# A gated linear unit on one core: the store of each tile issued behind the next tile's sigmoid instead of ahead of it

## The chip, the cores and the metric

The kernel runs on one core of one Trainium2 chip. The metric is the device time of one execution, in microseconds (us); lower is better. Beside it, one execution was recorded by the hardware profiler; the views of that record (the page, groups of instructions, waits, the chain of waits, stretches of time) are what the text reads.

## The reference

The input `x` has 8192 x 8192 float32 numbers. It is cut into a left and a right half of 4096 columns, and the left half is multiplied by the sigmoid of the right half:

```python
def reference(x: np.ndarray) -> np.ndarray:
    a, b = np.split(x, 2, axis=-1)
    return a * (1 / (1 + np.exp(-b)))
```

Every input number is read once (268 MB) and every output number written once (134 MB).

## The kernel before

The 8192 rows are cut into 32 tiles of 256 rows, two rows for each of the 128 partitions. A tile of `x` is one load of 8.39 MB (64 KB for each partition); its result is one store of 4.19 MB. There are two input buffers (`x_sb0`, `x_sb1`) and two output buffers (`o_sb0`, `o_sb1`); tile i uses number i mod 2 of each.

Nothing is scheduled by a tool: the order of instructions on each engine is the order in which the code writes them, and all waits are written by hand.

- SyncE issues the loads (`load`, L46 to L51, its DMA in L48). Load i+2 overwrites the input buffer of tile i, so it waits until multiply i is done. SyncE also issues the four part-stores of the last tile.
- ScalarE computes the sigmoid in place in the input buffer (L61) and waits for the load of its tile. ScalarE also issues the stores of tiles 0 to 30 (`store`, L78 to L89, its DMA in L82); store i waits until multiply i is done.
- VectorE multiplies the left half by the sigmoid into the output buffer (L72). Multiply i waits for sigmoid i and, by the same semaphore `ready[s]`, for store i-2, which reads the buffer that it overwrites:

```python
                self.to_ready[s] += 1 + (16 if i >= SLOTS else 0)
                waits.append((self.ready[s], self.to_ready[s]))
```

The first and the last tile are computed in four pieces each; the others in one sigmoid and one multiply. The loop in `trace` (L97 to L102) writes for each tile the sigmoid and the multiply, then load i+2, then the store of tile i. On ScalarE this makes the order sigmoid 0, store 0, sigmoid 1, store 1, and so on: a store's wait for its multiply stands ahead of the next tile's sigmoid.

The loads (SyncE's queue) and the stores (ScalarE's queue) run on the same 16 DMA engines.

Of the kernel before, what the change touches and what calls it, by code (L numbers as in the profile page):

```python
# [1 line left out]

# [4 lines left out]

P = 128
R = 2
SLOTS = 2  # L10


class _Program:

    def __init__(self, nc, x, out):
        self.nc = nc
        fp32 = mybir.dt.float32
        n_rows, n_cols = x.shape
        self.half = n_cols // 2  # L30
        self.n_tiles = n_rows // (P * R)
        self.x = x.rearrange("(n p r) m -> n p (r m)", p=P, r=R)
        self.out = out.rearrange("(n p r) m -> n p (r m)", p=P, r=R)
        self.xs = [nc.alloc_sbuf_tensor(f"x_sb{s}", [P, R * n_cols], fp32).ap() for s in range(SLOTS)]
        self.os = [nc.alloc_sbuf_tensor(f"o_sb{s}", [P, R * self.half], fp32).ap() for s in range(SLOTS)]
        self.loaded = [nc.alloc_semaphore(f"loaded{s}") for s in range(SLOTS)]
        self.ready = [nc.alloc_semaphore(f"ready{s}") for s in range(SLOTS)]
        self.product = nc.alloc_semaphore("product")
        self.sigmoid = nc.alloc_semaphore("sigmoid")
        self.arrived = nc.alloc_semaphore("arrived")  # L40
        self.last = nc.alloc_semaphore("last")
        self.to_ready = [0] * SLOTS
        self.products = self.sigmoids = self.lasts = 0
        self.done = {}

    def load(self, i, after=None):  # L46
        s = i % SLOTS
        ins = self.nc.sync.dma_start(out=self.xs[s][:, :], in_=self.x[i]).then_inc(self.loaded[s], 16)  # L48
        if i >= SLOTS:
            ins._wait_ge(self.product, self.done[i - SLOTS])  # L50
        return ins  # L51

    def work(self, i, pieces):

        nc, s = self.nc, i % SLOTS
        rows = self.xs[s].rearrange("p (r h m) -> p r h m", r=R, h=2)
        packed = self.os[s].rearrange("p (r m) -> p r m", r=R)
        waits = []
        for k, (r, c) in enumerate(pieces):
            b = rows[:, r, 1, c]  # L60
            sig = nc.scalar.activation(out=b, in_=b, func=mybir.ActivationFunctionType.Sigmoid)  # L61
            if k == 0:
                sig._wait_ge(self.loaded[s], 16 * (i // SLOTS + 1))
                self.to_ready[s] += 1 + (16 if i >= SLOTS else 0)
                waits.append((self.ready[s], self.to_ready[s]))
                sig.then_inc(self.ready[s], 1)
            else:
                self.sigmoids += 1
                waits.append((self.sigmoid, self.sigmoids))
                sig.then_inc(self.sigmoid, 1)  # L70
        for (r, c), wait in zip(pieces, waits):
            mul = nc.vector.tensor_mul(out=packed[:, r, c], in0=rows[:, r, 0, c], in1=rows[:, r, 1, c])  # L72
            mul._wait_ge(*wait)
            mul.then_inc(self.product, 1)
            self.products += 1
        self.done[i] = self.products

    def store(self, i, lo=0, hi=None, products=None):  # L78
        s, final = i % SLOTS, i == self.n_tiles - 1
        hi = R * self.half if hi is None else hi  # L80
        queue = self.nc.sync if final else self.nc.scalar
        ins = queue.dma_start(out=self.out[i][:, lo:hi], in_=self.os[s][:, lo:hi])  # L82
        ins._wait_ge(self.product, self.done[i] if products is None else products)
        if final:
            self.lasts += 16
            ins.then_inc(self.last, 16)
        else:
            ins.then_inc(self.ready[s], 16)
        return ins  # L89

    def trace(self):

        n, half = self.n_tiles, self.half
        whole = [(slice(0, R), slice(0, half))]
        fourths = [(slice(r, r + 1), slice(h * half // 2, (h + 1) * half // 2)) for r in range(R) for h in range(2)]
        self.load(1)
        for i in range(n):  # L97
            self.work(i, fourths if i in (0, n - 1) else whole)
            if i + SLOTS < n:
                self.load(i + SLOTS)  # L100
            if i < n - 1:
                self.store(i)  # L102
        for k in range(4):
            self.store(n - 1, k * half // 2, (k + 1) * half // 2, self.products - 3 + k)

    def close(self):


        nc, s = self.nc, (self.n_tiles - 2) % SLOTS
        for engine in (nc.scalar, nc.vector, nc.sync):  # L110
            engine.drain().then_inc(self.arrived, 1)  # L111
        nc.gpsimd.wait_ge(self.arrived, 3)
        nc.gpsimd.wait_ge(self.ready[s], self.to_ready[s] + 16)
        ids = sorted(h.num for h in (*self.loaded, *self.ready, self.product, self.sigmoid, self.arrived))
        assert ids == list(range(ids[0], ids[-1] + 1)) and self.last.num not in ids
        nc.gpsimd.sem_clear(range(ids[0], ids[-1] + 1))
        nc.gpsimd.drain()
        nc.sync.wait_ge(self.last, self.lasts).then_inc(self.last, -self.lasts)


def _launch_early(nc):

    SP = mybir.EngineType.SP
    entry, body = (b.instructions for b in nc.main_func.blocks[:2])
    load = next(i for i in body if i.engine == SP and i.opcode == "DMACopy")
    assert not load.sync_info.on_wait
    body.remove(load)
    where = next(k for k, i in enumerate(entry) if i.engine == SP and i.opcode == "Drain")  # L130
    entry.insert(where, load)


@with_exitstack
def kernel(
    ctx: ExitStack,
    tc: tile.TileContext,
    x: bass.AP,
    out: bass.AP,
):  # L140
    nc = tc.nc
    prog = _Program(nc, x, out)
    tc.info.no_tile_sem_insts.add(prog.load(0).ins.name)
    tc.close()
    tc.compile()  # L145
    _launch_early(nc)
    prog.trace()
    prog.close()


# [1 line left out]
_INS = ['x']  # L152
_OUTS = [((8192, 4096), 'float32')]


# [23 lines left out]
```

## Time and profile before

| what | value |
|---|---|
| time, median of 3 runs | 933.25 us (933.01 to 934.12) |
| the profiled execution: time, span | 933.08 us, 931.8 us |
| VectorE busy | 278.6 us (30%) |
| ScalarE busy | 226.8 us (24%) |
| bytes moved, mean rate over the span | 402.67 MB, 432 GB/s |
| loads, issue to landing (median) | 42.2 us |
| stores on ScalarE's queue, issue to landing (median) | 34.8 us |
| one sigmoid of a whole tile, one multiply | 7.03 us, 8.69 us |

How to read it: the span is the time from the first to the last instruction of the profiled execution; 1.3 us lie around it. "Busy" is the time in which an engine computed. "Issue to landing" counts from the instruction that issues a transfer until the last of its data is reported to have arrived, and so holds the time in which the transfer stood behind others. On the page the queue of SyncE is named q1 and that of ScalarE q10. DMA shares are those of 16 engines together; packets are counted where they end, so in short stretches a share may pass 1.

### The profile page before, as it was taken

Reading aid. Unit: us, or ns where it says so; the run is one execution under the profiler, and the core shown is the slowest. Engines: PE = TensorE matmul, PEld = TensorE weight load, DVE = VectorE, ACT = ScalarE, POOL = GpSimd, SP = SyncE. Lnnn points to the kernel's source line nnn. Section 1 sums busy time; section 2 is a strip of 40 time slices with the busy share of each in tenths; the row PEclk is TensorE's granted clock in tenths of the full one; section 3 lists DMA queues with packets and bytes.
Section 4 is the critical chain, followed back from the end, with each engine's and each line's share of the span. In section 5 each row is a group of like instructions: output and inputs, shape, how many; then the busy total and the mean of one; then the engine's idle time right before and its main releaser. Section 6 shows DMA issues by size and latency. Waiting matters only on the chain.

```text
span 931.8 us, 190 instructions
## 1 busy us (share of the span) xinstructions
DVE 278.6 (30%) x38; ACT 226.8 (24%) x39; POOL 0.2 (0%) x4
## 2 busy tenths in 40 slices
DVE  0333213333133331233312333123331233312333
ACT  1323330233311333113331133311333203332033
POOL 0000000000000000000000000000000000000000
DMA  9999999999999999999999999999999999999999
GB/s 405 428 450 428 422 456 405 450 428 428 450 421 435 428 436 442 428 428 450 450 405 430 442 456 428 412 463 408 450 428 428 450 408 447 428 428 450 426 429 405
DMA packets 9649, 402.67 MB, mean 432 GB/s; under 512 B 1072, under 2 KB 1072, under 8 KB 1072
## 3 DMA queue, kind: packets, MB, share of 16 engines
q1 hardware_dynamic: 5184, 272.63, 67.7%
q10 hardware_dynamic: 4464, 130.03, 32.3%
q14 instruction: 1, 0.01, 0.0%
HBM read 268.44 MB, written 134.22 MB: 432 GB/s over the span
## 4 chain that ended last, share of the span: by engine, by line
DMA 73%; DVE 15%; ACT 12%; DVEq 0%; issue 0%
DMA x_sb<-in_x_dram 73%; DVE o_sb L72 15%; ACT x_sb L61 12%; DVEq L111 0%
## 5 line engine op out<-in xcount | busy, mean ns | idle before, releaser
L72 DVE TENSOR_TENSOR o_sb<-x_sb 128x8192 f32<-128x8192 f32 (+1 forms) x38 | 278.6, 7344 | 647.1 <-ACT x_sb L61 647.1
L61 ACT ACTIVATE x_sb<-x_sb 128x8192 f32<-128x8192 f32 (+1 forms) x38 | 225.5, 5949 | 693.9 <-DMA x_sb<-in_x_dram 693.9
L61 ACT ACT_TABLE_LOAD x1 | 1.3, 1283 | 1.4 <-PEq L145 1.4
L163 POOL MEMSET const-bfloat16-1.0<- 128x1 bf16 x1 | 0.1, 102 | 0.0
L163 POOL MEMSET const-uint8-127<- 128x1 uint8 x1 | 0.1, 102 | 0.0
L163 POOL MEMSET const-float32-0.0<- 128x1 f32 x1 | 0.1, 99 | 0.2 <-issue 0.2
L163 POOL MEMSET const-float32-1.0<- 128x1 f32 x1 | 0.1, 99 | 0.0
## 6 DMA issues: line engine op xcount, KB each, us to landing
out_dram<-o_sb ACTq DMA_DIRECT2D x31, 4096.0 KB, 34.8
out_dram<-o_sb SPq DMA_DIRECT2D x4, 1024.0 KB, 5.7
x_sb<-in_x_dram SPq DMA_DIRECT2D x32, 42.2
```

The source lines that it names most:

```text
L61: sig = nc.scalar.activation(out=b, in_=b, func=mybir.ActivationFunctionType.Sigmoid)
L72: mul = nc.vector.tensor_mul(out=packed[:, r, c], in0=rows[:, r, 0, c], in1=rows[:, r, 1, c])
L163: nc = _bacc.Bacc("TRN2", target_bir_lowering=False, num_devices=1)
```

## The change

In the loop, the store of tile i-1 is written where the store of tile i stood, behind the work of tile i. For i = 30, the last turn that still has a store on ScalarE, both store 29 and store 30 are written. On ScalarE the order becomes sigmoid 0, sigmoid 1, store 0, sigmoid 2, store 1, ..., sigmoid 30, store 29, store 30, sigmoid 31. All waits, buffers, transfers and the order on the other engines are the same. Two blank lines in the class move the line numbers behind them by two.

```diff
@@ -98,7 +100,9 @@
             self.work(i, fourths if i in (0, n - 1) else whole)
             if i + SLOTS < n:
                 self.load(i + SLOTS)
-            if i < n - 1:
+            if 0 < i < n - 1:
+                self.store(i - 1)
+            if i == n - 2:
                 self.store(i)
         for k in range(4):
             self.store(n - 1, k * half // 2, (k + 1) * half // 2, self.products - 3 + k)
```

## The prediction

> **What bounds the kernel now.** I read the page first, parts 1 to 3: who is busy, and how evenly.
>
> ```profile
> DVE 278.6 (30%) x38; ACT 226.8 (24%) x39; POOL 0.2 (0%) x4
> ...
> DMA  9999999999999999999999999999999999999999
> ...
> q1 hardware_dynamic: 5184, 272.63, 67.7%
> q10 hardware_dynamic: 4464, 130.03, 32.3%
> ```
>
> VectorE and ScalarE work less than a third of the span; the 16 DMA engines never fall below nine tenths in any slice. The queue rows sharpen that: the packets of SyncE's queue (q1: all loads and the last tile's stores) take 67.7% of what 16 engines have in the span, those of ScalarE's queue (q10: the stores) 32.3%, together 100.0%. From the same rows, one load of 8.39 MB costs all 16 engines 0.677 x 931.8 x 8.39 / 272.63 = 19.4 us, one store of 4.19 MB 0.323 x 931.8 x 4.19 / 130.03 = 9.7 us: 29.1 us a tile.
>
> The chain of waits seems to say something else: it hops from load to sigmoid to multiply to load.
>
> ```profile
> by line: DMA x_sb<-in_x_dram 72.6%; DVE o_sb L72 14.7%; ACT x_sb L61 11.5%; DVEq L111 0.2%; issue 0.1%
> ...
> 160.74 7.04 ACT x_sb L61
> 167.80 8.70 DVE o_sb L72
> 176.52 42.13 DMA x_sb<-in_x_dram
> 218.67 7.04 ACT x_sb L61
> ```
>
> The loop is real (7.04 + 8.70 + 42.13 = 57.9 us for two tiles, 28.95 each), but the 42 us of a load are not 42 us of moving: 19.4 us would do. The rest is standing behind the load before it and alternating with a store. So the loop closes because the transfers are that slow, and its two compute links cost nothing. The stretches view confirms it between landings (columns: stretch and its length, then DVE, ACT and POOL busy, clock, DMA share, GB/s):
>
> ```profile
> 1.44:21.79 20.35, 0.00 (x0) 1.28 (x1) 0.00 (x0) 1.00 0.95 412
> 21.79:44.76 22.97, 8.90 (x4) 7.31 (x5) 0.00 (x0) 1.00 0.94 388
> ...
> 73.64:102.64 29.00, 8.69 (x1) 7.03 (x2) 0.00 (x0) 1.00 1.00 434
> ...
> 885.90:914.82 28.92, 8.69 (x1) 7.03 (x2) 0.00 (x0) 1.00 0.99 431
> 914.82:931.80 16.98, 8.90 (x4) 7.31 (x4) 0.00 (x0) 1.00 0.94 401
> ```
>
> Share 1.00 in the steady state. Only the ends are short of it (a stretch's share counts packets where they land, so I use it for long stretches): 5% of 20.35 us at the start, 6% of 16.98 us behind the last load, 1.0 us each. The change first acts at 32.66 us, where the store of tile 0 is issued now, so the start stays. What it could still win is about 1 us at the end.
>
> The second stretch also shows how the queues share. Load 1 needs 19.4 us alone and took 22.97; the 3.6 us more are three store packets (a store is 8 packets per engine, 1.21 us each), served between load packets of 2.43 us. The queues alternate packet by packet: while both hold work, loads get two thirds of the time, stores one third, just the ratio of their bytes.
>
> **The change, step by step.** Per tile the same 38 multiplies, 38 sigmoids and 67 DMAs; nothing is added or removed, only ScalarE's order moves: sigmoid i+1 now stands ahead of store i. No scheduler changes that; a listing of both kernels' instructions shows exactly this swap on ScalarE and nothing on the other engines.
>
> *What ScalarE gains.* Sigmoid i+1 no longer queues behind store i's wait for multiply i. It never suffered from it: ScalarE then idled another 21.9 us for the load (its 32 waits for loads sum to 693.9 us). Worth 0.
>
> *What the store loses.* Write T for the landing of load i+1. Now store i is issued 7.06 + 8.72 = 15.8 us behind its own tile's landing, at T - 13.2. After, it is issued behind sigmoid i+1, at T + 7.1: some 20 us later. The store's DMA is the only one that moves; SyncE's queue keeps its waits.
>
> *Start.* Load 1 is alone and lands at 21.79 + 19.4 = 41.2 (now 44.76). Store 0 goes out at 48.3. It reaches the engines 0 to 6.1 us later (the upper bound from store 0 now: issued at 32.66, none of its packets landed by 38.7, the first 16 by 40.1, so it joined at about 38.8). So load 2 runs alone 7.1 to 13.2 us, then at two thirds speed, and lands at 63.7 to 66.8 against 73.64 now: all loads shift 7 to 10 us ahead, and I take 8.5. Engines stay busy meanwhile: load 3 is issued at 41.2 + 15.8 = 57.0. From then each tile again moves one load and one store, 29.0 us.
>
> *The new wait.* Multiply i+2 writes the buffer that store i reads. Now store i lands 34.8 us after its issue, at T + 21.6, while multiply i+2 is due at T + 29.0 + 7.1 = T + 36.1: 14.5 us of slack. After, the same 34.8 us end at T + 41.9: the multiply waits 5.8 us behind its sigmoid. Bounds: 0 if the store takes only its shared 29 us; 12.7 us if it joins as late as 6.1 us. I take 6, by the 34.8 us row. Queued behind that multiply on VectorE is only the next one, 29 us away. Who waits for it: SyncE's load i+4, now issued 13.2 us ahead of the landing of load i+3, when the load queue would run empty; after, 7.2 us ahead. From issue to moving a load needs at most 2.4 us (load 0 lands at 21.79, 19.4 of it moving), so about 5 us of cover remain. At the 12.7 us bound the load queue would run dry for 2 us, and even that costs nothing: store i+1, issued before multiply i+2, holds up to 9.7 us of packets, so the engines then serve stores alone and catch up.
>
> The Trainium skill speaks against the move: the page "DMA: Bandwidth & Descriptors", section "Rules for kernel authors", wants a DMA issued early, compute done, and its semaphore waited on late. By that rule the store's 20 us of lost cover would show as lost time; the row of 100.0% says that delay in one queue is filled from the other.
>
> *End.* The last load lands at about 914.8 - 8.5 = 906.3, but the bytes skipped are still owed. The engines finish at about 931 now; from 906.3 that leaves 24.7 us of work: 9.7 for tile 31, 9.7 for store 30, 5.3 of store 29. Multiply 31 waits for store 29 till about 912.5 and its four pieces end at 921.4 (8.9 us as now); the last piece of the store is issued then (now 925.7) while the backlog lasts to 906.3 + 15.0 = 921.3 without pieces, and pieces 1 to 3 add 7.3 us. No hole opens; the end stays.
>
> Sum: 0 + 0 + 0. The profiled execution took 933.08 us (span 931.8 and 1.3 around it), the median of the runs is 933.25: I predict 933.2. Unknowns of a packet or so at the end: -0.9 to +1.5.
>
> **Rivals.** No change, forecast: 0.88. A change under 0.2% (1.9 us) is about what a measurement here cannot tell from none.
>
> *Slower: the circle through the output buffers runs both queues dry.* Store i lands, multiply i+2 (8.7) and the load's start (2.4) follow: 11.1 us until new load packets, covered by store i+1 (9.7) and the rest of load i+3. By my times that rest is 16 us of shared running, 10.7 us of packets. If it were gone when store i lands, 11.1 - 9.7 = 1.4 us would be idle in each of 29 tiles: 41 us, 974. It decides only if the multiply's wait grows from 6 to about 20 us, say because stores stand back behind queued loads. For: store landings of 34.8 us against 9.7 of work. Against: 34.8 is no more than alternation and the next store's tail. Chance 0.08.
>
> *Slower: the early-issue rule holds literally*, every multiply's 5.8 us lengthening its tile: 29 x 5.8 = 168 us, 1101. Against: the 42.1 us loads have that slack. Chance 0.01.
>
> *Faster: the last tile sets the end.* With the last load 8.5 us earlier and the chain behind it as now, 933.2 - 8.5 = 924.7. For: the chain of waits ends in load, sigmoid and multiply. Against: behind 914.82 the engines still carry 16 us of bytes, 0.94 busy. Chance 0.03.
>
> **How the numbers follow.** The forecast alone holds 0.88, so the range is its own: 933.2 with -0.9 and +1.5, 932.3 to 934.7. Faster 0.03, same 0.88, slower 0.08 + 0.01 = 0.09.
>
> **What would show it.** In the profile after: DMA nines throughout and the two queue shares again near 100%; stores to landing still 30 to 39 us; VectorE with waits for DMA of o_sb, some 6 us on about 29 multiplies (none now); landings about 8.5 us earlier from tile 2 on, still 29.0 us apart; the last load at about 906, the end at about 931.8. A DMA share of 0.95 in the middle, or loads over 30 us apart, would make it wrong towards slower; a span under 930 towards faster.

## The result, and the profile after

The changed kernel takes 949.81 us (median of 4 runs, 946.82 to 951.89) against 933.64 us: 1.0173 times as long, 95% interval 1.0158 to 1.0188. That is 16 us slower: less than 2%, but far clear of the noise. 933.2 had been forecast. The profiled execution took 951.89 us with a span of 950.6 us, 18.8 us more than before.

From its page: engines' busy time, the DMA row of the 40 slices, and the two queues (packets, MB, share of what 16 engines have in the span):

```profile
DVE 278.6 (29%) x38; ACT 226.8 (24%) x39; POOL 0.2 (0%) x4
...
DMA  9999999999999999999999999999999999999995
...
q1 hardware_dynamic: 5184, 272.63, 67.3%
q10 hardware_dynamic: 4464, 130.03, 31.7%
```

Packets and bytes are those of before. But the same loads took longer: 67.3% of 950.6 us are 639.8 us of all engines, against 630.8 before. The stores did not: 31.7% are 301.3 us, against 301.0. And the shares sum to 99.0%, not 100.0%: about 1% of the engines' time, 9.5 us, is empty. The last slice says where most of it is. In stretches between landings (as before: length, busy DVE, ACT, POOL, clock, DMA share, GB/s):

```profile
22.02:41.35 19.33, 8.89 (x4) 7.31 (x5) 0.00 (x0) 1.00 1.00 434
...
70.49:101.10 30.61, 8.69 (x1) 7.03 (x1) 0.00 (x0) 1.00 1.01 432
130.79:160.33 29.54, 8.69 (x1) 7.03 (x1) 0.00 (x0) 1.00 1.00 424
869.70:899.97 30.27, 8.69 (x1) 7.02 (x1) 0.00 (x0) 1.00 1.00 416
...
912.00:929.87 17.87, 3.72 (x1) 0.00 (x0) 0.00 (x0) 1.00 0.86 372
929.87:950.60 20.73, 8.90 (x4) 7.31 (x4) 0.00 (x0) 1.00 0.56 236
```

Load 1 alone lands in 19.33 us, as worked out. From load 3 on a tile takes 29.2 to 30.6 us, where before took about 29.0, and the share stays about 1.00: the engines are busy all the time and move less in it. Only at the end do they wait, 0.86 and 0.56: most have nothing left while the last load still lands.

The timeline (start, length, engine, line, instruction; ACTq is ScalarE issuing a transfer) shows something else that the prediction did not have:

```profile
41.35 7.03 ACT L63 ACTIVATE x_sb<-x_sb 128x8192 f32<-128x8192 f32 x1 [12.02 <-DMA x_sb<-in_x_dram]
41.35 0.38 ACTq L84 DMA_DIRECT2D out_dram<-o_sb  x1
48.41 8.69 DVE L74 TENSOR_TENSOR o_sb<-x_sb 128x8192 f32<-128x8192 f32 x1 [15.55 <-ACT x_sb L63]
70.49 7.03 ACT L63 ACTIVATE x_sb<-x_sb 128x8192 f32<-128x8192 f32 x1 [22.11 <-DMA x_sb<-in_x_dram]
70.50 0.34 ACTq L84 DMA_DIRECT2D out_dram<-o_sb  x1
```

The store behind a sigmoid is issued when the sigmoid STARTS (41.35, 70.50), not when it ends: ScalarE hands the transfer out while the sigmoid still runs. So stores go out at each load's landing.

**Packet by packet.** The trace also records each DMA packet: queue, size, start, duration. It does not number the engines, but packets follow each other within some nanoseconds, so an engine's row can be put together by matching ends to starts. (Where two engines' packets end at the same moment, the match can swap their rows, so sums for one engine are good to about 1 us.) L0 to L7 are the eight 64 KB packets of a load on one engine, S0 to S7 the eight 32 KB packets of a store, `|l|` and `|s|` the small packets that report a load's and a store's end; `*0.34` means that the packet took 0.34 us over its 2.42 us:

```
before, any engine     L5 |s| L6 S0 L7 S1 |l| S2 L0 S3 L1 S4 L2 S5 ...
after, slowest engine  |l| S7 L0 |s| L1*0.34 S0 L2 S1 L3*0.18 S2 L4 ...
after, other engines   |l| S5 L0 S6 L1 S7 L2 |s| L3 S0 L4 S1 L5 ...
```

(The lower two are the same 50 us, from 335 us on.) All the lost time lies in load packets that are drawn out. Past 60 us, 322 of the changed kernel's 3744 load packets take over 0.1 us too long, 0.39 us on average; before, one of 3760 does. Up to 790 us there are 198 of them, and some 170 of these stand where a store ends one load packet behind a load's end. Two engines are in that place in nearly all tiles, a third in some 19; the other 13 are in it for their first two to seven tiles, run ahead, so that a store ends two or three packets later in their row, and are then left in peace. The slowest engine has some 20 us of drawn-out packets from start to end, against some 2 us before; the difference of about 18 us is nearly all of the 18.8. A load has landed only when the slowest engine has it.

The other 124 come in the last tiles and mostly elsewhere. There the engines that ran ahead have emptied their store queue, and the load packet in service when the next store arrives is drawn out by 0.7 to 0.8 us on average (`L5 L6*0.78 S0 L7`). These engines have time to spare: most stand idle for 7 to 8 us before the last stores.

### The profile page after: what moved, and what is told of

It is laid out like the page before. It is cut to its first block, busy times and chain, and to the rows that moved or that the text cites. A ratio compares the mean times of both kernels' runs of the same rounds, so it can differ in the third digit from the quotient of the medians.

```text
span 950.6 us, 190 instructions
## 1 busy us (share of the span) xinstructions
DVE 278.6 (29%) x38; ACT 226.8 (24%) x39; POOL 0.2 (0%) x4
## 3 DMA queue, kind: packets, MB, share of 16 engines
q1 hardware_dynamic: 5184, 272.63, 67.3%
q10 hardware_dynamic: 4464, 130.03, 31.7%
## 4 chain that ended last, share of the span: by engine, by line
DMA 73%; DVE 14%; ACT 11%; DVEq 0%; issue 0%
DMA x_sb<-in_x_dram 73%; DVE o_sb L74 14%; ACT x_sb L63 11%; DVEq L115 0%
## 5 line engine op out<-in xcount | busy, mean ns | idle before, releaser
L63 ACT ACTIVATE x_sb<-x_sb 128x8192 f32<-128x8192 f32 (+1 forms) x38 | 225.5, 5949 | 709.0 <-DMA x_sb<-in_x_dram 709.0
## 6 DMA issues: line engine op xcount, KB each, us to landing
out_dram<-o_sb ACTq DMA_DIRECT2D x31, 4096.0 KB, 33.1
```

## The experiments

Ratios are to the kernel before, run on the same chip, with 95% intervals.

### Is it where the stores start, the compute beside them, or their lateness?

Theory W held that a store queue that has run empty costs at the next arrival; C that compute beside a store's start slows the loads; D that late or separate issue costs. In the first run store 0 alone is issued 7 us later, behind the END of sigmoid 1:

```diff
             if 0 < i < n - 1:
+                if i == 1:
+                    self.nc.scalar.drain()
                 self.store(i - 1)
```

> The changed kernel, but store 0 alone is issued behind the END of sigmoid 1 (a drain of ScalarE in front of it): about 7 us later, once. Theory W (an empty queue costs): when a store's packets reach a DMA engine whose store queue has run empty, the load packet in service is drawn out by some 0.6 us; in the changed kernel each store ends just before the next arrives, so this comes back in all 30 tiles (30 x 0.6 = 18 us). One later store 0 leaves a backlog that lasts: time about 933 to 935, loads 29.0 us apart. Rival C (a store that starts together with a sigmoid disturbs the loads in the buffers): 29 of 30 stores still start with a sigmoid, 947 to 952. Rival D (issuing loads and stores at different moments, or late stores, costs by itself): 947 to 952.

Measured: 933.48 us, 0.9998 (0.9989 to 1.0008). One store, moved once by 7 us, wins the whole loss back. The engines alternate packet by packet, so what the first store sets stays: in this run a store ends four load packets behind a load's end, 300 us on too. D falls.

In the second, sigmoid and multiply work on 64 columns only (`c = slice(c.start, c.start + 64)`, and the output buffers are filled with zeros once, so that most of the result stays zero):

> The changed kernel with sigmoid and multiply cut to 64 columns of each half row, the rest of the output stays zero; loads and stores in full. Theory W: stores are still issued at each load's landing, the store queue still runs empty before each: about 945 to 952. Rival C (sigmoid or multiply beside the store's start slows the loads): no compute to speak of, about 933. Rival D: 945 to 952, as W.

Measured: 949.26 us, 1.0158 (1.0131 to 1.0186), with almost no compute left. C falls.

In the third, every store waits for the end of the sigmoid, by the same `drain` without the `if`. This is the kernel that the prediction described:

> The changed kernel with each store issued behind the END of the sigmoid in front of it (a drain of ScalarE): what the prediction took the change to do, stores at T + 7.1. Theory W: store 0 joins later and ends later in the next load, the next store is issued about 5 us before the queue is empty: 933 to 935. Rival C: stores now start with the multiply instead of the sigmoid: 945 to 952 if the multiply disturbs as the sigmoid does. Rival D: stores are later still: 950 or more.

Measured: 933.58 us, 1.0001 (0.9992 to 1.0011). Its timeline and its waits (engine, line, what was waited for: us, times, longest):

```profile
66.77 7.03 ACT L63 ACTIVATE x_sb<-x_sb 128x8192 f32<-128x8192 f32 x1 [18.41 <-DMA x_sb<-in_x_dram]
73.88 0.34 ACTq L84 DMA_DIRECT2D out_dram<-o_sb  x1
81.16 8.69 DVE L74 TENSOR_TENSOR o_sb<-x_sb 128x8192 f32<-128x8192 f32 x1 [24.07 <-DMA out_dram<-o_sb]
```

```profile
DVE o_sb L74 <- DMA out_dram<-o_sb: 603.4, 30, 24.1
DVE o_sb L74 <- ACT x_sb L63: 39.5, 2, 23.9
```

The store is issued at 73.88, as sigmoid 2 ends, and multiply 2 starts at 81.16, 7.4 us behind the sigmoid, held by a store. Thirty multiplies are released by a store here, and it costs nothing.

In the fourth, each store waits until the one before it has landed, so that the queue is empty at every arrival:

```diff
             if 0 < i < n - 1:
+                if i > 1:
+                    self.nc.scalar.wait_ge(self.ready[i % SLOTS], self.to_ready[i % SLOTS])
                 self.store(i - 1)
```

> The changed kernel with each store (from store 1 on) waiting until the store before it has landed: the store queue is empty at every arrival, by force, and at a moment other than a landing of a load. Theory W: 28 to 31 empty arrivals of 0.6 us and more, 948 to 960. Rival C: stores start apart from the sigmoid, mostly without compute beside them: 933 to 940. Rival D: 948 or more.

Measured: 935.69 us, 1.0018 (1.0009 to 1.0028): 2 us, not 15 to 27. W misses. There is something in it, though. From store 2 on the queue is empty here for only some two load packets (5 us), and no packet is drawn out. Where it has been empty for longer, the rows do show a price: when store 0 arrives, the load packet in service is drawn out by 0.7 to 1.3 us on every engine, before the change too, and at the second arrival of this run, four load packets behind the store before it, by 0.5 us on average.

### An empty queue, or the place itself?

Here store 0 is issued as in the changed kernel, all others as before, so that the store queue is full when a store ends:

```diff
-            if i < n - 1:
+            if i == 1:
+                self.store(0)
+            if 0 < i < n - 1:
                 self.store(i)
```

> Store 0 is issued behind sigmoid 1, as in the changed kernel; all other stores are issued as in the kernel before, each right behind its own tile's multiply. So a store ends just where a load ends, as in the changed kernel, but the next store has been queued for some 15 us by then. Theory W (the queue must have run empty): 933 to 935. Rival P (the place of the stores relative to the loads' ends costs, full queue or not): 947 to 952. Rival D (late stores cost): 933 to 935.

Measured: 953.35 us, 1.0199 (1.0175 to 1.0223). W falls as the cause of the loss: the next store has been queued for some 15 us, and the loss is there in full. Its page:

```profile
q1 hardware_dynamic: 5184, 272.63, 68.1%
q10 hardware_dynamic: 4464, 130.03, 31.6%
```

68.1% of its span of 952.4 us are 648.6 us, 17.8 more than before, on all engines alike; the stores' 301.0 us are unchanged. No engine slips out of its place here; in the rows all 16 stay in it until the last load:

```
|l| S7 L0 |s| L1*0.56 S0 L2*0.28 S1 L3 S2 L4 S3 L5 S4 L6 S5 L7 S6 |l| S7 ...
```

Two load packets a tile are drawn out, 0.6 us together (18.0 us per engine over 30 tiles).

Three more runs price an empty queue by itself: loads alone, with no, one or two small stores a tile (one packet of 512 B on each engine).

> Base for a price: all loads in full, sigmoid and multiply cut to 64 columns of each half row and written in place, no stores but the four of the last tile (of zeros); most of the output is not written. 32 loads of 19.4 us, 2 at the start, the last stores: about 635 us by every theory.

> The base with one small store (16 partitions x 512 bytes, one packet for each DMA engine) per tile, issued at the landing of the tile's load, into a store queue that has been empty for about 19 us. Theory W: 31 arrivals in an empty queue at 0.6 to 1.0 us: 19 to 31 us over the base. Rival P: the bytes are nothing, so base plus less than 5 us.

> The base with two such small stores per tile, the second behind a sigmoid of 7 us, so that the queue is empty again: Theory W: 62 arrivals, twice the excess of one per tile, 37 to 62 us over the base. Rival P: base plus less than 5 us.

Measured, one run each: 635.15, 636.34 and 636.40 us. 31 arrivals of so small a packet in an empty queue cost 1.2 us together, another 31 no more. For a packet of 32 KB they decide nothing.

### What in that place?

Two theories of the place were on record. By B, ends of transfers on the two queues that fall near each other cost; by A, it is the addresses of the store and load packets that move side by side. To put a second end into the transfers, stores or loads were cut into two transfers of 64 partitions, with a control:

```diff
+            first = queue.dma_start(out=self.out[i][0:64, lo:hi], in_=self.os[s][0:64, lo:hi])
...
+        p = slice(0 if final else 64, P)
-        ins = queue.dma_start(out=self.out[i][:, lo:hi], in_=self.os[s][:, lo:hi])
+        ins = queue.dma_start(out=self.out[i][p, lo:hi], in_=self.os[s][p, lo:hi])
```

> The kernel with all stores behind the sigmoid's end (933.6 us), each store now issued as two transfers of 64 partitions, one behind the other, same bytes and packets. Theory B (a transfer's end and start on the store queue falling within two or three packets of a transfer's end and start on the load queue costs about 0.6 us): stores started 4 to 5 load packets into a load there; a split store has a second boundary 4 packets on, so on the load's own boundary: 945 to 955. Rival A (what costs is store packet k moving beside load packet k+1 of the 8, by address): the streams stay 4 packets apart, 933 to 937.

> The kernel with all stores behind the sigmoid's end (933.6 us), each load but the first now issued as two transfers of 64 partitions. Theory B: the new boundary in the middle of a load falls where the stores start: 945 to 955. Rival A: the streams stay 4 packets apart, 933 to 937.

> Control: the kernel before with each store issued as two transfers of 64 partitions. There a store starts between load packets 7 and 8, so the split falls between packets 3 and 4 of a load, just clear of its boundary. Theory B: 933 to 938. Rival A: 933 to 935. If splitting costs by itself (more transfers, shorter ones): as much here as in the kernel with late split stores.

Measured: 1018.34, 1479.01 and 986.99 us (1.0906, 1.5699 and 1.0591; the runs of the second scatter from 1458.51 to 1507.58, and its ratio is that of the two fastest). The control fails: cutting by partitions costs 54 us by itself and far more for loads, whose 64 KB packets take 4.47 us at the median instead of 2.42. These three decide nothing here.

Next the stores of the slow run went elsewhere in HBM, into a tensor of their own, 80 KB off a tile's start, so that the output holds the last tile only:

> The slow order with full queues (store 0 late, the rest as before, 953 us), the 31 large stores written to another tensor in HBM, 80 KB off any tile's start; the output holds only the last tile. Theory B (ends of transfers on both queues within two or three packets): nothing changes, 948 to 954. Rival A (addresses of the store's packets beside those of the load's): another alignment, so most of the 20 us goes, 933 to 940.

Measured: 952.96 us, 1.0208 (1.0193 to 1.0223). At this other place the loss is the same.

Then, again with store 0 alone late, the rows of a tile were dealt so that load packets are 32 KB and store packets 16 KB (`"(n r p) m -> n p r m"`), and the same was done in the order of before:

> The same slow order with the tile's rows dealt to the partitions so that a partition's two rows lie 128 rows apart: 16 load packets of 32 KB and 16 store packets of 16 KB per engine and tile, same bytes, same ends of transfers. Theory B: the ends still fall together, 945 to 955 against its own control. Rival A: other addresses side by side, no reason for a loss at the same place, within 5 us of its control.

> Control: the kernel before with the same dealing of rows. Twice the packets at half the size, order of stores as before: 933 to 940 by both theories.

Measured: 935.28 and 935.31 us (1.0018 and 1.0017). No loss; but in this trace a store ends three of the smaller load packets behind a load's end, not one, so B's condition wasn't met, and the run decides less than planned.

The rest vary only the moment of store 0. It goes out behind the first of two half sigmoids of tile 1 (other stores as in the changed kernel), or behind the first of four quarters (others as before). The lines that both have in common:

```diff
                 sig.then_inc(self.ready[s], 1)
+                if i == 1:
+                    nc.scalar.drain()
+                    self.store(0)
```

> The changed kernel with store 0 alone issued 3.6 us behind the landing of load 1 (behind the first of two half sigmoids) instead of at once or 7 us behind. Stores then start one or two packets further from the load's end. Theory B: between the two, 933 to 943, nearer 935 if three packets are apart enough. Rival A gives no order between the phases: anything from 933 to 955.

> All stores as in the kernel before, but store 0 issued 1.9 us behind the landing of load 1 (behind the first of four quarter sigmoids). A store's end should fall two load packets behind a load's end (one: 953 us; three: 933 us). Theory B (ends on both queues near each other cost, on either side): 933 to 943. Rival S (only a store that starts in a load's first packets costs): 933 to 943 as well; this run gives the width.

Measured: 933.12 us (0.9999, 0.9990 to 1.0009) and 933.41 us (1.0000, 0.9990 to 1.0009). In their rows a store ends three and two load packets behind a load's end, and past 60 us one load packet of some 3740 is late in each.

Last, store 0 between before's moment and the changed one, behind a sigmoid on an unused buffer (7100 and 4300 columns):

> All stores as in the kernel before, but store 0 issued about 6.3 us later (a sigmoid on an unused buffer in front of it): a store's end should fall together with a load's end, within the same packet. Theory B: 945 to 960. Rival S: the store starts between the load's first and second packet, 945 to 960.

> As the run before this, with some 3.9 us: a store's end should fall one load packet AHEAD of a load's end, the next store starts with the load's last packet. Theory B: 940 to 955. Rival S: 933 to 936.

Measured: medians of 939.06 us (1.0041, 1.0017 to 1.0066) and 934.65 us (1.0028, 1.0002 to 1.0053), runs scattered from 933.4 to 943 (and one of the first at 960.23, which the ratio leaves out). In the profiled execution of each, most engines came out at the same place, an end beside an end:

```
S6 L7 S7 |l| |s| L0 S0 L1 S1 L2 S2 ...   most engines of both runs
|l| S7 L0 |s| L1*0.15 S0 L2*0.11 ...     first run, two engines that slipped by a packet
S7 L6 |s| L7 S0 |l| S1 L0 S2 L1 ...      second run, three engines
```

In the first run 14 engines keep that place with nothing drawn out, and the two that slipped lose 6 us each over 29 tiles. In the second, 13 keep it and lose 1 to 3.6 us each, mostly in the last tiles; on the other three a store ends one load packet ahead of a load's end in every tile, the case that this run was to make, and past 60 us none of their packets is drawn out.

B expected the worst here and finds little; S, that a store must not start in a load's first packets, falls too, since S0 stands right behind L0. What is left is narrow: one load packet between the ends (load first) costs the engine that stands there 0.2 us a tile where two engines do, and 0.6 where all 16 do; two, three or four behind cost nothing, one ahead costs nothing, nor does before's place, two packets ahead, and ends side by side cost nothing in one run and little in the other.

## Why the prediction was wrong, point by point

**The step that failed** is "After, it is issued behind sigmoid i+1, at T + 7.1", and with it "From then each tile again moves one load and one store, 29.0 us". The store is issued at T. I had costed the move by the sigmoid's end, though no row of before shows ScalarE issuing a store behind a running sigmoid without another wait; the honest bounds were T and T + 7.1. At T + 7.1 the forecast holds (933.58 us), and it is enough that store 0 alone goes out then (933.48). That this moment leads to a harmless place is luck, since the prediction did not ask for the place. With store 0 at T a store ends one load packet behind a load's end, where two load packets are drawn out; a tile takes (929.87 - 70.49) / 29 = 29.6 us instead of 29.0, 18 us over the 29 tiles. I took the rate of the engines as fixed, because before shows 1.00 and 434 GB/s in every tile; but before stands in one place only.

The record before the change already held a drawn-out packet, in the 3.6 us by which load 1 was late. The prediction took them for "three store packets". In the rows only two store packets (2.4 us together) stand inside load 1; most of the rest is its packet L6, in service when store 0 arrives, which takes 0.8 to 1.1 us too long on every engine. So a load packet does not always take 2.42 us, and a sum in packets of fixed length could not show what moving the stores does to them.

**Right, once the store leaves at T + 7.1**: load 2 lands at 66.77 (63.7 to 66.8 forecast), the last at 907.75 (906.3), the multiply waits 7.4 us (6, bounds 0 and 12.7), the end does not move. So do the reasons: ScalarE gains nothing, delay in one queue is filled from the other, the skipped bytes are owed at the end. (The 38 multiplies, 38 sigmoids and 67 DMAs that the prediction has "per tile" are those of the whole run; nothing hangs on it.)

**In the changed kernel itself** the new wait does not show: each store is issued 7 us sooner than forecast and lands 33.1 us later at the median, and VectorE waits for ScalarE alone:

```profile
ACT x_sb L63 <- DMA x_sb<-in_x_dram: 709.0, 32, 23.6
DVE o_sb L74 <- ACT x_sb L63: 662.2, 32, 24.0
```

ScalarE's wait for loads grew from 693.9 to 709.0, the loss as it looks from there.

**The rivals.** Dry queues were not the cause of the loss: the share stays about 1.00 until the last tile, and the loss is there in full where the next store is always queued (953.35 us). The early-issue rule of the Trainium skill ("DMA: Bandwidth & Descriptors", "Rules for kernel authors") has the sign right, but its reason, a fixed setup cost that overlaps, is not what runs here show: the kernel whose stores are later still loses nothing. Of the signs that were named, a DMA share of 0.95 in the middle did not come, and loads over 30 us apart came only near the start and the end (30.61 and 30.27). No rival had the packets themselves get longer, so the range had no room for 16 us. I had read alternation as a ratio only, and not asked what stays fixed by it: the place of one queue's ends in the other's.

**Open.** Why that place costs was not settled. Compute, an empty queue and lateness are out as the cause of the loss, and so is the one other place in HBM that was tried. A is not tested for the addresses in the buffers; against it speaks that mostly two load packets of eight are drawn out, though all eight move beside store packets. Nor is it shown why a store that arrives in a queue long empty draws a packet out. The Trainium skill says in the same page's section "Queues, rings and completion order" that an engine takes turns between queues packet by packet, which the rows show, and that the report of a transfer's end lands only after all earlier writes of that engine, in any queue. Two reports with a store and a load packet between them could hinder each other by that; but two reports side by side cost little or nothing, and no run here shows it.

## What to carry to other kernels

In these runs, while both DMA queues stayed full, the order in which they alternate was set once and kept. Where a change to transfers costs time that no wait explains, look in the packet records where a store ends relative to a load's end, and if load packets are drawn out there, move the first store once by a packet or two rather than reorder every tile. A transfer written behind a compute instruction on the same engine is not behind its end: here the store was issued when the sigmoid started (both at 41.35 us), and with a drain it was issued when the sigmoid ended (73.88). And a share of 1.00 says that the DMA engines are busy, not that they move as much as they can: multiply each queue's share by the span and compare it with the same bytes elsewhere.

## What the runs showed of the hardware that was not expected

- A load packet of 64 KB, 2.42 us in tens of thousands of records, takes up to 3.3 us in the changed kernel, and once 3.9 us in the run with the other place in HBM, where a store's end follows a load's end with one store and one load packet between them; store packets keep 1.21 us in that place.
- One engine in that place sets the pace, since a load has landed with its slowest engine: about 18 us on one engine cost 18.8, though the mean of the loads' packet time over all engines grew by 9.
- When the first store arrives, the load packet in service takes 0.7 to 1.3 us longer on all 16 engines, in the kernel before as in the changed one; behind a queue that was empty for only two load packets it does not.
- Loads cut into two halves of 64 partitions took 4.47 us a packet: 1479.01 us instead of 933.58 for the same bytes.
- 62 small stores, one packet of 512 B on each engine, into a queue that had run empty between them cost 1.25 us in 635.
